# Cutting the last six megabytes of weights into transfers of 120 and of 8 partitions

## The chip, the cores and the metric

The kernel runs on one core of a Trainium2 chip. The metric is the device time of one execution in microseconds (us). A core has five engines that run beside each other: TensorE (PE, matrix products; its weight loads are shown as PEld), VectorE (DVE), ScalarE (ACT), GpSimd (POOL) and SyncE (SP, which here only starts transfers). Transfers between the chip's main memory and the core's own memory of 128 partitions are moved by 16 DMA engines that all transfers share.

## The reference

One inference step of a one-layer backbone over two streams of 128 tokens (T = 256 tokens in all) with model width 1024. The part that matters here is the last one, a mixture of 32 experts, of which every token takes four:

```python
def expert_step(acc, e):
    w_gu_e, b_gu_e, w_down_e, b_down_e, w_tok = e
    g, u = jnp.split(t @ w_gu_e + b_gu_e, 2, axis=-1)
    g = jnp.minimum(g, SWIGLU_LIMIT)
    u = jnp.clip(u, -SWIGLU_LIMIT, SWIGLU_LIMIT)
    act = (u + 1.0) * g * jax.nn.sigmoid(SWIGLU_ALPHA * g)
    out = act @ w_down_e + b_down_e
    return acc + w_tok[:, None].astype(out.dtype) * out, None
```

Each expert has w_gu (1024 by 2048) and w_down (1024 by 1024) in float32, 12 MB together. After the experts come the residual sum and a final norm over the 1024 channels. Before them stands a mixer (a state-space scan and a convolution branch), which the change doesn't touch.

## The kernel before

The mixture of experts takes the last two thirds of the time. The loop `for e in range(NE)` calls `expert(e)` for the 32 experts in order. The order of TensorE's instructions is the order in which the program writes them; the other engines' order is set by a scheduler.

**How an expert's weights come in.** The 12 MB of an expert are six units of 2 MB. Units c = 0 to 3 are 256 rows of w_gu each, units c = 4 and 5 are 512 rows of w_down each. Unit u = 6e + c goes to place u mod 11 of a ring of eleven places (`place`), so the kernel holds nearly two experts at a time. A unit is a tile of 128 partitions by 16 KB: partition p holds k consecutive rows of the matrix (k = 2 for w_gu, 4 for w_down), and `t[:, i]` is the i-th of them. The eleventh place is made of two pieces of 1 MB, whose tiles have names that end in a and b (w_0a, w_0b for unit c = 0); for expert 31 that is unit c = 0.

`load_unit(u, h)` (from line 377) starts the transfers of a unit on SP's queue, line 390. A unit goes as one transfer of 2 MB over all 128 partitions. Only for the last expert (e = 31) a unit of w_down goes as two transfers of 1 MB, each with half of the k rows. `load_pieces` (line 413) calls it for the units that are due: in `expert(e)`, after the second product of expert e - 1 has been written, the units up to number 6e + 10; behind it in the program come a branch (line 1335) to an extra pass for experts with more than 64 tokens of a stream, and the first product of expert e. A transfer can start when the place's last reader is done and when SP has come to it. Each transfer announces its landing on one of eight counters, taken in turn, and SP starts a transfer only when the one that used its counter before has landed.

**What an expert computes.** `expert_up` (line 1224) multiplies the expert's 64 gathered tokens by w_gu: 8 steps k over the 1024 input channels, 8 matmuls in each, so 16 matmuls for a unit, and 4 more for the bias at line 1229. `expert_act` (lines 1237 to 1241, on DVE and ACT) makes the activation, `transposed` (lines 1277 and 1280) turns it, and `down_products` (line 1290) multiplies by w_down: 8 steps of 4 matmuls, step k with row k of the eight that the two w_down units hold on a partition. `keep_y` (line 1298) copies the result out, and products at line 1305 add it to the tokens xT.

For experts 0 to 30 the second product and the adding of a pair are done while the next expert's activation is under way, so TensorE has work in it. After the last expert, `finale` (from line 1456) does what is left: the second product of expert 31, the last adding (lines 1469 and 1168), the squares and their sums, the norm, and five transfers of the output from line 1503.

The lines that the change touches are these of `load_unit`:

```python
        step = k // 2 if e == NE - 1 and c > 3 else k
        for i in range(0, k, step):
            npc_ins[0] = nc.sync.dma_start(t[:, i:i + step], src[:, i:i + step])
        return [t[:, i] for i in range(k)]
```

Of the kernel before, what the change touches and what calls it, by code (L numbers as in the profile page):

```python
# [20 lines left out]
P = 128  # L21
# [4 lines left out]
NE = 32  # L26
# [37 lines left out]
def hybrid_step(ctx, tc, A):  # L64
    nc = tc.nc
# [100 lines left out]
    for i in range(4):  # L166
        r = slice(32 * i, 32 * i + 32)
# [196 lines left out]
    npc_ins, last_early = [None], [None]  # L364
    w_gu, w_dn = A["w_gu"], A["w_down"]

    def place(i, name, h):

        if i < NUNIT - 2:
            return mx[i + 1].tile([P, 4 * D], F32, name=name, tag="w")  # L370
        if i == NUNIT - 2:
            return ypool.tile([P, 4 * D], F32, name=name, tag="y")
        if h:
            return keep.tile([P, 2 * D], F32, name=f"{name}b", tag="xn", bufs=1)
        return mx[0].tile([P, 2 * D], F32, name=f"{name}a", tag="w")

    def load_unit(u, h):

        e, c = divmod(u, 6)
        src, k = (w_gu[0, e, 256 * c:256 * c + 256], 2) if c < 4 else (w_dn[0, e, 512 * (c - 4):512 * (c - 3)], 4)  # L380
        src = src.rearrange("(p k) n -> p k n", k=k)
        t = place(u % NUNIT, f"w{e}_{c}", h)
        if u % NUNIT == NUNIT - 1:
            k //= 2
            src = src[:, h * k:h * k + k]
        t = t.rearrange("p (k n) -> p k n", k=k)

        step = k // 2 if e == NE - 1 and c > 3 else k
        for i in range(0, k, step):
            npc_ins[0] = nc.sync.dma_start(t[:, i:i + step], src[:, i:i + step])  # L390
        return [t[:, i] for i in range(k)]

    def parts(u):
# [6 lines left out]
    def early_pieces(n):  # L400

        with tc.issue_after(last_load[0].ins):
            for _ in range(n):
                u, h = early.pop(0)
                ready[u, h] = load_unit(u, h)
                last_early[0] = npc_ins[0]
# [6 lines left out]
    def load_pieces(n):  # L413

        for u in range(nun[0], min(n, 6 * NE)):
            for h in parts(u):
                pieces.setdefault(u // 6, []).extend(ready.pop((u, h), None) or load_unit(u, h))
        nun[0] = max(nun[0], n)
# [1169 lines left out]
```

## Time and profile before

| | us |
|---|---|
| median of 3 runs | 1441.97 |
| lowest and highest of them | 1440.35 and 1442.50 |
| the profiled execution, its own time | 1441.85 |
| its span, from the first to the last instruction | 1440.0 |

| engine | busy, us | share of the span |
|---|---|---|
| PE | 1341.3 | 93% |
| DVE | 591.6 | 41% |
| ACT | 337.8 | 23% |
| POOL | 110.2 | 8% |

The time of an execution is its span and 1.85 us around it. A busy share is a mean over stages that are limited by different things, so it doesn't tell what a change in one stage is worth: for that, the stretch in which the change lies is looked at, and in it what each wait ends with. Times in the rows below are counted from the start of the span.

### The profile page before, as it was taken

The page shows a single profiled execution, that of the slowest core. Times are in us where ns is not written, and L with a number is a line of the kernel's source. Part 1 is how long each engine was busy: PE and PEld are TensorE (multiplying, and loading weights), DVE is VectorE, ACT ScalarE, POOL GpSimd, SP SyncE. Part 2 cuts the span into 40 slices and gives each one's busy share as a digit, 9 for nine tenths or more (in the row PEclk, how much of TensorE's full clock was granted, in tenths as well). Part 3 has the DMA queues.
Part 4 walks back from the last instruction along what each step waited for, and adds up shares of the span by engine and source line. Part 5 has one row for each costly group of instructions (what it writes and reads, how often), then busy time and mean ns, then how long its engine had stood idle before and what let it go on. Part 6 is the DMA issues. An engine that isn't in the chain of part 4 may idle for free. (4 is left out here: it accounts for less than half of the span.)

```text
span 1440.0 us, 20912 instructions
## 1 busy us (share of the span) xinstructions
PE 1341.3 (93%) x8545; PEld 795.8 (55%) x8545; DVE 591.6 (41%) x1265; ACT 337.8 (23%) x636; POOL 110.2 (8%) x121
## 2 busy tenths in 40 slices
PE   6999999999999899999999899999999999989995
PEld 3888888898999643434434344344333443434432
DVE  4856789898776322123122213213212213123123
ACT  2534565565664100000000001000000010000001
POOL 1112313431002100000000000000000000000001
PEclk9999999999999899999999999999999999999998
DMA  9996666556877799999999999999999999999981
GB/s 367 275 275 175 217 211 236 206 211 205 312 289 264 274 401 425 424 423 426 422 426 425 413 419 425 422 426 425 424 425 424 426 423 427 422 426 424 425 369 37
DMA packets 83711, 506.55 MB, mean 352 GB/s; under 512 B 6866, under 2 KB 34130, under 8 KB 51410
## 3 DMA queue, kind: packets, MB, share of 16 engines
q1 hardware_dynamic: 80658, 497.71, 86.8%
q10 hardware_dynamic: 2880, 6.60, 1.3%
q8 instruction: 100, 1.64, 0.5%
q14 instruction: 73, 0.60, 0.1%
HBM read 498.26 MB, written 5.64 MB: 350 GB/s over the span
## 5 line engine op out<-in xcount | busy, mean ns | idle before, releaser
L291 DVE TENSOR_TENSOR wl<-win,wh 128x1024 fp32r<-128x1024 f32 (+1 forms) x84 | 101.3, 1217 | 36.5 <-ACT wh L290 24.0
L290 ACT CAST wh<-win 128x1024 fp32r<-128x1024 f32 (+1 forms) x84 | 83.9, 1009 | 73.2 <-PE pbc L318 19.2
L1482 POOL TENSOR_TENSOR sql<-sql 128x256 f32<-128x256 f32 x3 | 2.2, 730 | 943.0 <-PE pcl L1469 942.6
L702 POOL TENSOR_TENSOR m<-m_half,adt 128x512 fp32r<-128x512 f32 x32 | 43.2, 1370 | 89.2 <-PE pss L705 89.2
L318 PE MATMUL pxs<-hT,wh 128*128 128x256 f32 x256 | 37.5, 291 | 0.0
L318 PE MATMUL pz<-hT,wh 128*128 128x256 f32 x256 | 37.3, 291 | 0.0
L318 PE MATMUL pgt<-hT,wh 128*128 128x256 f32 x256 | 36.0, 287 | 0.6 <-ACT wh L290 0.6
L318 PE MATMUL pbc<-hT,wh 128*128 128x256 f32 x256 | 35.6, 287 | 0.0
L318 PEld LDWEIGHTS pxs<-hT,wh 128*128 128x128 f32 x256 | 32.5, 190 | 3.6 <-issue 2.8
L318 PE MATMUL pso<-yhl,wh 128*128 128x256 f32 x256 | 34.1, 284 | 0.0
L318 PEld LDWEIGHTS pz<-hT,wh 128*128 128x128 f32 x256 | 33.0, 193 | 1.8 <-issue 1.8
L318 PEld LDWEIGHTS pgt<-hT,wh 128*128 128x128 f32 x256 | 32.4, 191 | 2.6 <-issue 1.9
L318 PEld LDWEIGHTS pbc<-hT,wh 128*128 128x128 f32 x256 | 32.2, 190 | 1.9 <-issue 1.7
L318 PEld LDWEIGHTS pso<-yhl,wh 128*128 128x128 f32 x256 | 32.1, 192 | 0.0
L318 PE MATMUL pglu<-hT,wh 128*128 128x256 f32 x192 | 27.1, 293 | 0.0
L318 PEld LDWEIGHTS pglu<-hT,wh 128*128 128x128 f32 x192 | 25.2, 199 | 0.8 <-issue 0.5
L215 PE MATMUL pm<-ada,sc__170 128*32 128x512 f32 x80 | 15.0, 807 | 9.9 <-DMA ada<-in_w_ada 9.9
L291 DVE TENSOR_TENSOR wl<-wso,wh 128x1024 fp32r<-128x1024 f32 x16 | 19.5, 1221 | 7.5 <-ACT wh L290 7.3
L686 DVE SCALAR_TENSOR_TENSOR gd<-gm,dtT,gd 128x128 f32<-128x128 f32 x64 | 21.3, 381 | 1.7 <-ACT gd L685 1.3
L685 ACT ACTIVATE gd<-gm,dtT 128x128 f32<-128x128 f32 x64 | 20.8, 415 | 4.3 <-DVE gm L676 4.3
L290 ACT CAST wh<-wso 128x1024 fp32r<-128x1024 f32 x16 | 16.7, 1045 | 14.3 <-PE pso L318 10.8
L318 PE MATMUL pwo<-mhl,wh 128*128 128x256 f32 x128 | 18.9, 290 | 0.2 <-DVE mhl L996 0.2
(1094 smaller groups left out, 2640.4 us busy)
## 6 DMA issues: line engine op xcount, KB each, us to landing
w<-in_w_gu SPq DMA_DIRECT2D x116, 2048.0 KB, 30.3
w<-in_w_down SPq DMA_DIRECT2D x57, 2048.0 KB, 26.3
win<-in_w_in_pack SPq DMA_DIRECT2D x38, 1024.0 KB, 5.6
ada<-in_w_ada SPq DMA_DIRECT2D x10, 1024.0 KB, 10.1
wso<-in_w_ssd_out SPq DMA_DIRECT2D x8, 1024.0 KB, 6.8
im<-dru SPq DMA_DIRECT2D x16, 312.0 KB, 9.5
wcf<-in_w_conf_out SPq DMA_DIRECT2D x4, 1024.0 KB, 9.3
wo<-in_w_o SPq DMA_DIRECT2D x4, 1024.0 KB, 9.2
```

Of the source, the lines that this page charges most:

```text
L215: PE.matmul(out[32 * j:32 * j + 32, :], sc_[:, 4 * r + j, 6 - 2 * c:38 - 2 * c], part[:, j, :], start=(start and r == 0), stop=(stop and r ...
L290: S.copy(hi[:, ks, 0:m], w[:, ks])
L291: V.tensor_tensor(lo[:, ks, 0:m], w[:, ks], hi[:, ks, 0:m], ALU.subtract)
L318: last_wo[0] = PE.matmul(out, w[:, k, 0:n], m[:, k, :], start=first and i == 0, stop=last and i == len(order) - 1, skip_group_check=True)
L685: S.activation(gd[s][:, h, :], gm[:, 0, s, :], AF.Copy, scale=dtT[:, 0, s, c0:c0 + 1])
L686: V.scalar_tensor_tensor(gd[s][:, h, :], gm[:, 1, s, :], dtT[:, 0, s, 32 + c0:33 + c0], gd[s][:, h, :], op0=ALU.mult, op1=ALU.add)
L702: G.tensor_tensor(m4[d], m_half[:, d, None, None, :].to_broadcast([P, 2, 4, 64]), ac[d], ALU.mult)
L1482: G.tensor_tensor(sq[:, 0], sq[:, 0], sq[:, k], ALU.add)
```

## The change

For the last three units of expert 31 (c = 3, the last of w_gu, and c = 4 and 5, its w_down: 6 MB) every transfer over 128 partitions is replaced by two: one over partitions 0 to 119, and behind it on the same queue one over partitions 120 to 127. The five transfers of these units become ten. Places, tiles, rows and everything that computes stay as they are.

```diff
         step = k // 2 if e == NE - 1 and c > 3 else k
+
         for i in range(0, k, step):
-            npc_ins[0] = nc.sync.dma_start(t[:, i:i + step], src[:, i:i + step])
+            for r in (slice(0, 120), slice(120, P)) if e == NE - 1 and c > 2 else (slice(0, P),):
+                npc_ins[0] = nc.sync.dma_start(t[r, i:i + step], src[r, i:i + step])
         return [t[:, i] for i in range(k)]
```

## Rows read from the trace of the kernel before

**Rows 1.** Chain that ended last, in order of time: start, us, what.
```profile
1331.39 38.74 DMA w<-in_w_gu
1370.20 35.24 DMA w<-in_w_gu
1405.48 3.65 PE e31pgu L1224 x16
```

**Rows 2.** Timeline of PE, 1360 to 1424: start, us, what, idle before.
```profile
1364.43 14.27 PE L1224 MATMUL e30pgu<-w,xg 128*64 128x512 f32 x64 [0.29 <-PEq L1335]
...
1385.38 7.09 PE L1290 MATMUL e30py<-w,e30aT 128*64 128x512 f32 x32 [0.68 <-ACT e30aT L1280]
...
1394.95 1.91 PE L1224 MATMUL e31pgu<-w_0b,xg 128*64 128x512 f32 x8
1396.66 3.63 PE L1224 MATMUL e31pgu<-w,xg 128*64 128x512 f32 x16
1400.58 3.65 PE L1224 MATMUL e31pgu<-w,xg 128*64 128x512 f32 x16 [0.29 <-DMA w<-in_w_gu]
1405.48 3.65 PE L1224 MATMUL e31pgu<-w,xg 128*64 128x512 f32 x16 [1.25 <-DMA w<-in_w_gu]
...
1412.40 0.72 PE L1277 MATMUL e31pat<-ident,e31gm 128*128 128x128 f32 x4 [2.83 <-DVE e31gm L1241]
1413.80 8.67 PE L1290 MATMUL e31py<-w,e31aT 128*64 128x512 f32 x32 [0.68 <-ACT e31aT L1280]
```

**Rows 3.** Stretches: busy of each engine, PEclk, DMA share, GB/s.
```profile
1223.00:1390.00 167.00, 155.85 (x772) 66.78 (x772) 39.34 (x102) 13.98 (x24) 0.00 (x0) 1.00 1.01 424
...
1394.00:1402.00 8.00, 7.71 (x38) 2.80 (x36) 0.00 (x0) 0.00 (x0) 0.00 (x0) 1.00 0.68 274
1402.00:1404.00 2.00, 2.00 (x12) 0.50 (x8) 0.00 (x0) 0.00 (x0) 0.00 (x0) 1.00 0.20 82
1406.00:1412.00 6.00, 3.57 (x20) 1.06 (x16) 2.41 (x4) 0.63 (x1) 0.00 (x0) 1.00 0.06 26
1414.00:1416.00 2.00, 2.00 (x6) 0.56 (x6) 0.00 (x0) 0.00 (x0) 0.00 (x0) 0.50 0.03 12
```

**Rows 4.** Timeline of SP, 1331 to 1390: the starts of transfers.
```profile
1331.39 2.81 SPq L390 DMA_DIRECT2D w<-in_w_gu  x2
1338.78 6.21 SPq L390 DMA_DIRECT2D w<-in_w_down  x2
1349.56 0.33 SPq L390 DMA_DIRECT2D w_0a<-in_w_gu  x1
1354.47 0.33 SPq L390 DMA_DIRECT2D w_0b<-in_w_gu  x1
1359.37 11.16 SPq L390 DMA_DIRECT2D w<-in_w_gu  x3
1375.06 12.56 SPq L390 DMA_DIRECT2D w<-in_w_down  x4
...
1379.93 0.33 SPq L390 DMA_DIRECT2D w<-in_w_down  x1
1384.99 0.33 SPq L390 DMA_DIRECT2D w<-in_w_down  x1
1387.30 0.33 SPq L390 DMA_DIRECT2D w<-in_w_down  x1
```

**Rows 5.** DMA issues at 1354.47, 1375.06 and 1387.30: KB, us to landing.
```profile
w_0b<-in_w_gu SPq DMA_DIRECT2D x1, 1024.0 KB, 35.3
w<-in_w_down SPq DMA_DIRECT2D x1, 1024.0 KB, 32.9
w<-in_w_down SPq DMA_DIRECT2D x1, 1024.0 KB, 28.1
```

**Rows 6.** DMA issues on an emptier queue: the output's last, and w_in_pack's.
```profile
o_tokens<-xT SPq DMA_DIRECT2D x2, 128.0 KB, 2.0
win<-in_w_in_pack SPq DMA_DIRECT2D x38, 1024.0 KB, 5.6
```

## The prediction

> **What bounds the kernel now.** The chain of waits, read backwards from the end, says that the last thing TensorE (PE) waits for in the expert loop is a transfer: unit c = 3 of expert 31, started at 1370.20 and landed 35.24 us later, at 1405.44, and PE goes on at 1405.48 [rows 1]. From there everything to the end hangs on PE and the short work of the other engines. The timeline of PE shows how little that wait costs: of the four units of w_gu of expert 31, the third makes PE wait 0.29 us (to 1400.58) and the fourth 1.25 us [rows 2]. The second product, e31py, is not waiting for weights at all: it starts at 1413.80 when its input e31aT is ready.
>
> The table of stretches says why that transfer is late [rows 3]. Up to 1390 the 16 DMA engines are full (share 1.01, 424 GB/s, so 26.5 GB/s each). From 1394 to 1402 the share is 0.68, from 1402 to 1404 it is 0.20, and from 1406 to 1412 it is 0.06 at 26 GB/s: one engine out of sixteen, alone. So fifteen engines have carried all their part of the 6 MB by about 1404, and one is more than 11 us behind. A transfer counts as landed when its last engine is done, so the late engine sets every landing. The four transfers of w_down bear this out: the first lands at 1375.06 + 32.9 = 1407.96, the last at 1387.30 + 28.1 = 1415.40 [rows 4, 5]. That is 7.44 us for three more transfers, 2.48 us each; a sixteenth of 1 MB, 65,536 bytes, in 2.48 us is 26.4 GB/s, the speed of one engine. It carries exactly the share of 8 partitions out of 128.
>
> The same rows tell when the fifteen have c = 3. Their slowest ends near 1403.5, and the four transfers of w_down behind c = 3 take 4 x 2.48 = 9.9 us, so c = 3 is done on them by about 1393.6, 11.8 us before it counts as landed.
>
> **The change, part by part.**
>
> *Which engine is relieved.* Eight partitions are one engine's part of 128. If the 120 partitions are carried by fifteen engines, 8 partitions each as now, and the engine left out is the late one, it gets nothing of c = 3, 4 and 5 from those. The other eight partitions of c = 3 are 131,072 bytes. Spread over eight engines that is one partition of 16 KB each, 0.62 us at 26.4 GB/s; carried by one engine it is 4.96 us. The trace of before has no transfer of 8 or of 120 partitions, so I bound both: the landing of c = 3 comes between 1393.6 + 0.6 = 1394.2 (late engine left out, eight rows spread) and 1405.44 + 4.96 = 1410.40 (late engine not left out, and all eight rows on it). I take the lower end: the cut at 120 leaves fifteen whole shares of the kind that the landings show.
>
> [...]
>
> *c = 3 in time.* What PE waits for then is c = 2, a transfer that isn't touched: PE still starts that unit's 16 matmuls at 1400.58. Without a wait a unit takes 16 matmuls at the spacing of the groups before, 1396.66 - 1394.95 = 1.71 us for 8, so 3.42 us [rows 2]. The last unit starts at 1404.00 instead of 1405.48: **-1.48 us**. Landed at 1394.2, it has nearly 10 us to spare.
>
> *The queue of SP.* Transfers take eight counters in turn, and a start waits for the landing of the eighth transfer before it. The chain shows it: the one started at 1331.39 lands at 1370.13, and the next start is 1370.20; from 1331.39 there are 2 + 2 + 1 + 1 + 2 = 8 starts before that [rows 1, 4]. With ten transfers in place of five, the same starts reach less far. 120 of c = 3 starts at 1370.20 as before, its 8 at 1375.06; the first half of c = 4 at 1379.93 and 1384.99, the second at 1387.30 and (landing of w_0b, 1354.47 + 35.3) 1389.8. The first half of c = 5 needs the landings of c = 1 (a 2 MB share, 4.96 us, after w_0b: 1394.8) and of c = 2 (1400.5). Then the last two start behind each other near 1401.2 and 1401.8, since the counters they need, those of c = 3, are free. All of it is late compared with 1375.06 to 1387.30 now. On an emptier queue 1 MB lands in 5.6 us and 128 KB in 2.0 us [rows 6], so the last lands near 1401.2 + 5.6 = 1406.8. The fifteen engines by themselves would need 1403.5 plus an eighth of 14.9 us on those that carry extra rows, 1405.4. So 1407 at the latest.
>
> That is hidden by the first product and the activation: e31py then starts at 1412.3, and its steps 6 and 7, which read the last half, come 6/8 of 7.09 us later, at 1417.6. Ten us of cover. If the cover were gone, each us of delay would be a us of the end. Nobody is queued behind SP's waits but the output's transfers at 1434. Nor does PE wait for SP at the branch of line 1335: PE passed it and began e30pgu at 1364.43, and SP, which has the starts of units 185 to 190 ahead of that branch, did them until 1379.93 [rows 2, 4]. The five added starts cost SP 0.33 us each in time that it spends waiting.
>
> *More waits on PE.* Each of five units has two landings to wait for instead of one; both are long past, and no row shows a price apart from the idle times. Nothing, with 0.1 us each as an upper bound.
>
> *The clock.* [...] So e31py takes 8.67 us where e30py takes 7.09, at full clock: 1.58 us lost [rows 2]. [...] I take the clock to fall as before, because the longest idle is the one that stays; the other end is that the 1.58 us come back as well.
>
> **The sum.** The profiled execution has 1441.85 us, 0.12 below the median of 1441.97. 1441.85 - 1.48 = 1440.37, so **1440.4 us**, 0.1% less. That is within 0.2% (2.9 us), which is about what a measurement of this kernel can tell from no change.
>
> **The rivals.**
>
> *The clock comes back too.* [...] Against it: 2.83 us without a matmul remain. 1440.37 - 1.58 = 1438.8, just past 0.2%.
>
> *Not relieved.* The late engine is one of the fifteen. For it: nothing in the trace names it. Then c = 3 lands at 1405.44 as now and, if the engine also carries one of the eight rows, 0.62 us later, with PE behind it: 1441.9 to 1442.5. The last half would start after that landing and be done near 1417, before 1419.7, when it would be needed. The time doesn't change.
>
> *Slower: fifteen engines that don't reach the pace of sixteen.* Place: the two units of w_down. If a transfer of 120 partitions runs at half speed, then from the slowest engine's start on c = 3 (1393.6 - 4.96 = 1388.6), with 9.9 us for c = 3 and 5.0 for each half, and 0.6 and 0.3 for the small ones, c = 3 is there at 1399.1 (still in time), the halves at 1404.4, 1409.6, 1414.9 and 1420.2. e31py waits for the last and does its last quarter, 1.77 us: 1422.0 against 1413.80 + 8.67 = 1422.47 now. So at half speed the gain is just gone, and slower still costs: at a third of full speed c = 3 comes at 1404.1, the halves every 7.7 us, the last at 1434.9, and the end 14 us later, 1456. Against it: an engine alone moves 26 GB/s, as each does among sixteen, so they don't take from each other now [rows 3]. The same arithmetic gives 1444.6, just past 0.2%, at 0.45 of full speed.
>
> [...]
>
> **Chances.** Forecast 0.64, clock back 0.13, not relieved 0.17, too slow 0.06. Faster by over 0.2% is most of the clock's case and a little of the forecast's, as the three runs lie 2.15 us apart: 0.12. Slower by over 0.2% is the last case: 0.06. Within 0.2% is the rest, 0.82. The range goes from the clock's case to that of no relief with the added row: 1438.6 to 1442.6.
>
> **What would show it.** In the profile after: the idle before the last 16 matmuls of e31pgu gone and that before the group ahead still there, ending near 1400.6; the DMA share falling to 0.06 only before that, and no engine alone after 1407; SP's starts at the times given, the last two past 1400; e31py starting near 1412.3 without a DMA wait. It is wrong if c = 3 still lands after 1404.0 (the wrong engine was relieved), if e31py waits for w_down (too slow), or if PE's clock there is 1.00 (the clock's case).

## The result

The kernel after takes 1464.87 us (median of 4 runs, 1459.46 to 1467.86) against 1441.6 us before (4 runs on the same chip, 1440.35 to 1442.5): ratio 1.0155, 95% interval 1.0132 to 1.0178, so 1.6% **slower**. The forecast was 1440.4 us, in a range of 1438.6 to 1442.6, and no measurable change. The profiled execution of after takes 1465.07 us with a span of 1463.2, 23.2 more than that of before.

The new loop moves the lines behind it by two: L1226, L1292 and L392 of after are L1224, L1290 and L390 of before. The chain that ended last (start, us, what) shows where the time is:

```profile
1357.84 44.47 DMA w_0b<-in_w_gu
...
1402.35 3.34 PE e31pgu L1226 x8
1405.69 7.73 another core or an unknown queue
...
1413.46 5.09 PE e31pgu L1226 x16
1418.55 4.64 another core or an unknown queue
...
1423.23 5.32 PE e31pgu L1226 x16
```

The chain of before has one late transfer at its end, c = 3 [rows 1]. That of after has three, and all three are transfers that the change doesn't touch: w_0b, c = 1 and c = 2. The two stretches of "another core or an unknown queue" are waits for a landing that the chain gives to no instruction; the timeline of PE (start, us, what, and in brackets the idle before it and what ended it) names them:

```profile
1367.18 10.52 PE L1226 MATMUL e30pgu<-w,xg 128*64 128x512 f32 x48 [0.29 <-PEq L1337]
1378.42 3.65 PE L1226 MATMUL e30pgu<-w,xg 128*64 128x512 f32 x16 [0.72 <-DMA w<-in_w_gu]
...
1393.15 3.65 PE L1292 MATMUL e30py<-w,e30aT 128*64 128x512 f32 x16 [0.73 <-DMA w<-in_w_down]
...
1397.54 1.94 PE L1226 MATMUL e31pgu<-w_0a,xg 128*64 128x512 f32 x8
1402.35 3.34 PE L1226 MATMUL e31pgu<-w_0b,xg 128*64 128x512 f32 x8 [2.88 <-DMA w_0b<-in_w_gu]
1413.46 5.09 PE L1226 MATMUL e31pgu<-w,xg 128*64 128x512 f32 x16 [7.78 <-DMA w<-in_w_gu]
1423.23 5.32 PE L1226 MATMUL e31pgu<-w,xg 128*64 128x512 f32 x16 [4.69 <-DMA w<-in_w_gu]
1428.97 3.65 PE L1226 MATMUL e31pgu<-w,xg 128*64 128x512 f32 x16 [0.41 <-DMA w<-in_w_gu]
...
1437.28 8.56 PE L1292 MATMUL e31py<-w,e31aT 128*64 128x512 f32 x32 [0.68 <-ACT e31aT L1282]
```

Read beside [rows 2], the waits before e31pgu are 2.88 + 7.78 + 4.69 + 0.41 = 15.76 us instead of 0.29 + 1.25 = 1.54: +14.22. Behind the three long waits the granted clock is lower as well: the groups of w_0b, c = 1 and c = 2, which took 1.91, 3.63 and 3.65 us at a granted clock of 1.00, take 3.34, 5.09 and 5.32 (clock 0.59 at 1402 to 1406, and 0.50 at 1410 to 1414 and 0.67 at 1424 to 1428 in the table below), together +4.56. With the 0.73 us ahead of the second half of e30py that is 19.51 us.

To keep apart what an execution lost earlier, I take the time from the start of e30pgu to the start of e31py: 1413.80 - 1364.43 = 49.37 us before [rows 2], and 1437.28 - 1367.18 = 70.10 after, +20.73. The other 2.75 us of the profiled execution were lost by 1367.18, ahead of the first changed transfer (SP starts it at 1373.52), so they aren't the change's. Such differences are usual: e30pgu starts between 1360.89 and 1367.18 in the nine traces of this kernel and its variants. Nor is the 0.72 us inside e30pgu the change's: that transfer landed at 1378.38, before the rate of the transfers fell (next table). That leaves 20.0 us, of which 19.51 are named above.

The table of stretches (length, busy of PE, PEld, DVE, ACT, POOL, granted clock, DMA share, GB/s), to be read beside [rows 3]:

```profile
1226.00:1374.00 148.00, 138.90 (x696) 59.37 (x694) 31.61 (x78) 12.77 (x22) 0.00 (x0) 1.00 1.01 425
...
1378.00:1382.00 4.00, 3.58 (x18) 1.27 (x20) 0.00 (x0) 0.00 (x0) 0.00 (x0) 1.00 1.04 440
1382.00:1386.00 4.00, 3.53 (x18) 2.14 (x14) 3.67 (x10) 0.63 (x1) 0.00 (x0) 1.00 1.04 254
1386.00:1390.00 4.00, 2.81 (x14) 1.80 (x16) 4.00 (x15) 0.59 (x1) 0.00 (x0) 1.00 0.90 197
...
1398.00:1402.00 4.00, 1.47 (x8) 0.33 (x4) 0.15 (x1) 0.01 (x1) 0.00 (x0) 1.00 0.94 203
...
1410.00:1414.00 4.00, 0.54 (x2) 0.29 (x4) 0.00 (x0) 0.00 (x0) 0.00 (x0) 0.50 0.64 164
...
1422.00:1424.00 2.00, 0.77 (x2) 0.30 (x4) 0.00 (x0) 0.00 (x0) 0.00 (x0) 0.80 0.07 25
1424.00:1428.00 4.00, 4.00 (x16) 1.12 (x12) 0.00 (x0) 0.00 (x0) 0.00 (x0) 0.67 0.12 39
```

Two columns must be read together here. From 1382 to 1402 the DMA share stays at 0.9 and more, so the engines look about as full as ever, but they move 197 to 254 GB/s instead of the 425 of the first row: the packets take longer. The median packet of 16 KB (one row of a unit) took 0.614 us before, 1.2 us between 1384 and 1423 of after, and 0.617 us from 1424 to 1428 (six packets), when the late engine was nearly alone again (a share of 0.12).

The landings, which the trace keeps one by one (sixteen for a transfer of 128 partitions), say which packets PE waits for (us; "late" is a transfer's last landing, "next" the last but one of its sixteen, or of its fifteen and eight in the last two rows):

```
                        before: next    late   |  after: next     late
w_down, 2nd of e30           1374.01  1384.93  |       1377.60  1393.10
w_0a                         1376.49  1387.28  |       1380.08  1397.08
w_0b                         1378.97  1389.77  |       1382.56  1402.31
c = 1                        1383.88  1394.69  |       1391.83  1413.42
c = 2                        1388.79  1400.54  |       1402.16  1423.19
c = 3 (120 rows in after)    1393.70  1405.44  |       1410.27  1428.22
c = 3, 8 rows                                  |       1409.61  1428.83
```

The late engine stands in every row of after, in the transfer of 120 partitions (15 landings) and in that of 8 (8 landings): their last landings come 5.03 us and 5.64 us behind its c = 2, when the others are done by 1410.27. And its own steps through old, uncut transfers have about doubled: from w_0a to w_0b to c = 1 to c = 2 it takes 5.23, 11.11 and 9.77 us, against 2.49, 4.92 and 5.85. In before the same landings show that the lag has built up slowly: the last engine comes 6.2 us behind the last but one at 1092, 8.9 at 1218, 10.8 at 1395 and 11.8 with c = 2.

The landings also show when this starts and what it isn't. The first five engines have c = 2 at 1382.89 to 1383.61 and come to the cut rows then, just where the GB/s falls; the first four landings of the 120 rows follow at 1392.67 to 1393.04, nearly ten us later, where the same five had taken 4.9 us from c = 1 to c = 2. The late engine hadn't begun on cut rows: its own share of the 120 comes after its c = 2 and takes 5.03 us (1423.19 to 1428.22), the old pace, as the others are nearly done by then. So a share of cut rows isn't slow in itself: packets are slow while many engines carry such shares (1.2 us against 0.617), and those of old transfers are slow with them (11.11 us for c = 1 against 4.92).

### The profile page after: what moved, and what is told of

It reads as the page before. It is cut to its first block, busy times and chain, and to the rows that moved or that the text cites. A ratio compares the mean times of both kernels' runs of the same rounds, so it can differ in the third digit from the quotient of the medians.

```text
span 1463.2 us, 20921 instructions
## 1 busy us (share of the span) xinstructions
PE 1348.1 (92%) x8545; PEld 797.2 (54%) x8545; DVE 589.9 (40%) x1265; ACT 337.7 (23%) x636; POOL 109.8 (8%) x121
## 3 DMA queue, kind: packets, MB, share of 16 engines
HBM read 498.26 MB, written 5.64 MB: 344 GB/s over the span
## 5 line engine op out<-in xcount | busy, mean ns | idle before, releaser
L1226 PE MATMUL e31pgu<-w,xg 128*64 128x512 f32 x48 | 14.1, 738 | 12.9 <-DMA w<-in_w_gu 12.9
L688 DVE SCALAR_TENSOR_TENSOR gd<-gm,dtT,gd 128x128 f32<-128x128 f32 x64 | 21.3, 381 | 1.7 <-ACT gd L687 1.2
L290 ACT CAST wh<-wso 128x1024 fp32r<-128x1024 f32 x16 | 16.7, 1046 | 14.3 <-PE pso L318 10.8
```

The costliest lines, as they stand in the source:

```text
L290: S.copy(hi[:, ks, 0:m], w[:, ks])
L688: V.scalar_tensor_tensor(gd[s][:, h, :], gm[:, 1, s, :], dtT[:, 0, s, 32 + c0:33 + c0], gd[s][:, h, :], op0=ALU.mult, op1=ALU.add)
L1226: PE.matmul(banks[i][m * q:m * q + m, 0:wd], xg[:, k, :], w[k][:, c0:c0 + wd], start=(k == 0), stop=False, skip_group_check=True)
```

## The experiments

Three things changed at once: fifteen and eight engines instead of sixteen (by the landings), ten starts instead of five, and rows cut otherwise. The theory to test is that the cut itself slows the engines, through where the rows go. The rivals are the number of engines, the number of starts and counters, and the addresses that are read.

**bench_rows.** No model at all: thirteen groups of eight loads of 16 KB per partition into one tile, each group after the one before has landed. The outputs are copies of that tile.

```python
buf[:, i] <- src[i][0:128]                  # L82, L85, L118
buf[0:120, i] <- src[i][0:120]              # L88; L91 with 112, L94 with 64
buf[0:120, i] <- far[i][0:120]              # L97; L100 with 128: rows 64 KB apart
buf[0:120, i] <- row[i] to 120 partitions   # L103; L106 with 128: one row, repeated
buf[0:8, i] <- src[i][0:8]                  # L109
buf[0:32:4, i] <- src[i][0:8]               # L112
buf[0:128:16, i] <- src[i][0:8]             # L115
```

> No model at all: thirteen groups of eight loads into one buffer of 128 partitions, each group begun when the one before has landed; 16 KB to a partition in every load; the outputs are copies of the buffer. Groups of 128 rows (2 MB) should take 39.6 us at 26.5 GB/s per engine. [...] Theory B (reading: each engine's source becomes one run of 128 KB in main memory and these collide): 120 contiguous rows about 79 us, but 120 rows from one repeated row about 40 us, and the three groups of eight rows are alike. Theory C (neither; the slow pace is the big kernel's own, from many small starts): 120 rows take 40 us, 112 rows 35 us, 64 rows 20 us.

The timeline of SP gives the start of each group; a group's time is the distance to the next start. Below it, the page's row of GB/s in 40 slices of 15.1 us.

```profile
42.97 4.13 SPq L85 DMA_DIRECT2D buf<-in_w_gu  x8
85.27 3.75 SPq L88 DMA_DIRECT2D buf<-in_w_gu  x8
165.41 3.75 SPq L91 DMA_DIRECT2D buf<-in_w_gu  x8
223.37 5.04 SPq L94 DMA_DIRECT2D buf<-in_w_gu  x8
266.83 3.62 SPq L97 DMA_DIRECT2D buf<-in_w_gu  x8
344.83 3.94 SPq L100 DMA_DIRECT2D buf<-in_w_gu  x8
386.70 3.66 SPq L103 DMA_DIRECT2D buf<-in_w_gu  x8
466.69 4.16 SPq L106 DMA_DIRECT2D buf<-in_w_gu  x8
508.74 2.66 SPq L109 DMA_DIRECT2D buf<-in_w_gu  x8
530.04 5.42 SPq L112 DMA_DIRECT2D buf<-in_w_gu  x8
539.18 4.85 SPq L115 DMA_DIRECT2D buf<-in_w_gu  x8
551.99 4.01 SPq L118 DMA_DIRECT2D buf<-in_w_gu  x8
```

```profile
GB/s 358 429 346 419 431 304 199 207 200 207 165 265 267 265 211 207 206 170 205 207 208 210 168 432 433 301 203 202 205 195 172 412 428 284 49 96 167 432 431 334
```

128 rows take 42.3 us and run at 430 GB/s. 120 rows, less data, take 80.1 us (about 200 GB/s). The source doesn't matter: 120 rows that lie 64 KB apart take 78.0 us, one row sent 120 times 80.0, and the same two with 128 rows 41.9 and 42.05. The number of engines isn't the reason either: 112 rows land with sixteen announcements, as 128 do, and still take 58.0 us (265 GB/s; theory C had 35). 64 rows, half the data, take 43.5 us (206 GB/s). What is left is where the rows go, and which engine carries which. Eight rows from the same source (8 rows posted 8 landings in after) show that the place counts. Into adjacent partitions the eight loads take 21.3 us, into partitions 16 apart 12.8, into partitions 4 apart 9.1. By the landings one load follows another in 2.41 us (131,072 bytes: 54 GB/s) and in 1.29 us (102 GB/s); 4 apart they come as fast as SP starts them, 0.67 us apart.

So the pace depends on which partitions are written: 54 GB/s for eight adjacent ones and 102 for eight that lie 16 apart, from the same rows. And of the four cuts of a unit only that of 128 rows is fast: 430 GB/s, against 200 for 120 rows, 265 for 112 and 206 for 64. Why a place has the pace it has is shown by no run, nor which rows an engine gets of 120 or 112; that such transfers run at 200 and 265 GB/s instead of 430 is measured.

**probe_late.** The kernel before, with eight loads of a few bytes behind the last weights. The 8 rows of after posted 8 landings; if a load of n rows uses n engines, and fewer rows use the first of the same engines, the smallest n with a late landing names the engine. Nothing of the model reads them.

```diff
+        if u == 6 * NE - 1:
+            probe = place((u + 2) % NUNIT, "probe", 0)
+            for j, n in enumerate((7, 4, 2, 6, 1, 3, 5, 8)):
+                nc.sync.dma_start(probe[0:n, 16 * j:16 * j + 16], A["w_dt"][0:n, 0, 0:16])
+                if n > 6:
+                    G.tensor_copy(probe[0:n, 512 + 16 * j:512 + 16 * j + 16], probe[0:n, 16 * j:16 * j + 16])
```

> The kernel before, with eight tiny loads of 7, 4, 2, 6, 1, 3, 5 and 8 rows behind the last weights, into memory that nothing of the model reads, and GpSimd reading the one of 7 and the one of 8 rows. A load of n rows goes over n engines if the changed kernel's landings are read rightly (8 landings for 8 rows). If engines are taken from the lowest number, the late engine is the n-th for the smallest n whose load is late. Theory A (the late engine is the eighth): all loads of 1 to 7 rows land 2 to 3 us after their start, that of 7 near 1392, and only that of 8 comes after the last weights, near 1415. Theory B (one of the first seven): the load of 7 rows is late too, near 1415, and the smaller ones tell which. The time stays within 0.2% of before.

1439.44 us in one execution, with before at 1442.29: the probes cost nothing that shows. The landings of 7, 6, 5 and 4 rows, started at 1387.21, 1402.83, 1410.32 and 1392.06, were complete at 1412.99 to 1413.53, when the late engine had the last weights down (1412.80); those of 3, 2 and 1 rows within 1.4 us of their start. GpSimd's copy behind the 7 rows shows it in its timeline:

```profile
1413.13 0.19 POOL L396 COPY probe<-probe 7x16 f32<-7x16 f32 x1 [931.71 <-DMA probe<-in_w_dt]
```

Four rows are the smallest load that lands late, so, counted that way, the late engine is the fourth, and not the eighth as in theory A. It is among the fifteen and among the eight, as the landings of after show without any counting.

**ten_full.** Ten transfers for c = 3 to 5, like the change, but each over all 128 partitions.

```diff
-        step = k // 2 if e == NE - 1 and c > 3 else k
+        step = 1 if e == NE - 1 and c > 2 else k
```

> Ten transfers for the last three units as in the change, but each of 128 partitions, cut by rows of the matrix (1 MB for c = 3, 0.5 MB for c = 4 and 5). If the price of the change came from ten starts on eight counters: 1455 to 1465. If it came from how 120 and 8 rows lie on engines and partitions: no price, 1440 to 1442, and as c = 3 comes in two halves its wait shrinks, so up to 1.5 us less than before.

Faster by 0.2%: 1438.93 us against 1442.29, ratio 0.9977 [0.9965, 0.9989]; the median is 3.4 us less, more than the 1.5 expected, but the interval reaches down to 1.6. Ten starts and their counters are not the price. In the timeline of PE the wait before c = 3 is gone (32 matmuls in one run), which is the term that the prediction counted on:

```profile
1397.93 7.09 PE L1224 MATMUL e31pgu<-w,xg 128*64 128x512 f32 x32 [0.30 <-DMA w<-in_w_gu]
...
1408.28 1.10 PE L1277 MATMUL e31pat<-ident,e31gm 128*128 128x128 f32 x4 [2.83 <-DVE e31gm L1241]
1410.06 9.16 PE L1290 MATMUL e31py<-w,e31aT 128*64 128x512 f32 x32 [0.68 <-ACT e31aT L1280]
...
1425.68 2.41 PE L196 MATMUL pssl<-one,sql 128*128 128x1 f32 x20 [0.71 <-POOL sql L1482]
```

**c3_halves.** Only c = 3 in two halves over 128 partitions, six starts.

```diff
-        step = k // 2 if e == NE - 1 and c > 3 else k
+        step = k // 2 if e == NE - 1 and c > 2 else k
```

> Before, with unit c = 3 of expert 31 in two transfers of 128 partitions and 1 MB, as its w_down has them already; six starts instead of five. The late engine is left as it is. The first half lands about 2.5 us before the second, the second where c = 3 landed, so TensorE does 8 of the 16 matmuls while it waits: the wait of 1.25 us shrinks to 0.3 us or less. Theory A (the whole gain of the ten transfers is this wait): 1.0 to 1.5 us less than before, ratio 0.9990 to 0.9993, as the ten had within their interval. Rival (w_down in quarters had a share in the gain): no change that shows, ratio 0.9995 to 1.0005.

1440.67 against 1441.61 us, ratio 0.9990 [0.9979, 1.0000]: no difference clear of noise, and the interval holds both what theory A and what its rival expected. The same run of 32 matmuls without a wait stands in its trace, and from e30pgu to e31py it takes 48.37 us, as ten_full takes 48.41: 1.0 less than before.

```profile
1401.19 7.09 PE L1224 MATMUL e31pgu<-w,xg 128*64 128x512 f32 x32 [0.28 <-DMA w<-in_w_gu]
```

**cut_112.** The change with the cut at 112, so that both parts divide by sixteen (112 rows posted sixteen landings in bench_rows).

```diff
-            for r in (slice(0, 120), slice(120, P)) if e == NE - 1 and c > 2 else (slice(0, P),):
+            for r in (slice(0, 112), slice(112, P)) if e == NE - 1 and c > 2 else (slice(0, P),):
```

> The change with the cut at 112 instead of 120: 112 rows are 7 for each of 16 engines, 16 rows are one for each, so no engine is left out and none carries more than its sixteenth. [...] If the price is that fifteen and eight engines are used, unevenly: 1440 to 1443.

1457.25 us in one execution, against 1442.29 of before: not the 1440 to 1443 of a price for using fifteen and eight engines. It is the same picture as the change; first a stretch (1380 to 1384, 209 GB/s), then PE's longest wait, the one before c = 1:

```profile
1380.00:1384.00 4.00, 3.33 (x18) 1.76 (x18) 3.23 (x13) 0.58 (x1) 0.00 (x0) 1.00 1.00 209
```

```profile
1405.85 5.74 PE L1225 MATMUL e31pgu<-w,xg 128*64 128x512 f32 x16 [8.36 <-DMA w<-in_w_gu]
```

**cut_64, c3_only, c5_only.** The same edit with the cut at 64; with the cut at 120 for c = 3 alone (`c == 3`); and for c = 5 alone (`c == 5`), which has no bytes that e31pgu reads.

> The change with the cut at 64: two transfers of 64 partitions each, over 16 engines, four partitions on each. In the load test 64 rows went at 206 GB/s, half of 128 rows. [...]

> The change for unit c = 3 alone; c = 4 and 5 as before. [...] Rival (the price is that of c = 4 and 5 behind it, or of ten starts): 0 to 2 us more. If the late engine had been left out, it would be 1.5 us less.

> The change for unit c = 5 alone, the last 2 MB, for which TensorE doesn't wait in the kernel before. [...] Rival (each transfer of 120 or 8 rows is slow in itself only): c = 5 lands later and nothing waits for it but the last steps of e31py: 0 to 2 us more.

One execution each, beside 1441.61 us of before: 1464.92, 1460.09 and 1451.19, so +23.3, +18.5 and +9.6 us. All three are slower, as they must be if the cut rows slow other transfers, and the 0 to 2 us of the rivals of c3_only and c5_only are out. What sets the three sizes is shown by no run. c5_only is the one that tells most. The stretches show the GB/s fall while c = 1 and c = 2 are on their way, and the timeline of PE shows what it waits before c = 1, c = 2 and c = 3: 7.58 us instead of the 1.54 of [rows 2]. With the 2.92 us that the group of c = 2 takes longer (6.57 instead of 3.65, with the granted clock at 0.50 from 1408 to 1412 and 0.74 from 1412 to 1416) that is the whole difference of 8.9 us in the measure below:

```profile
1384.00:1388.00 4.00, 3.33 (x18) 1.79 (x19) 3.29 (x13) 0.59 (x1) 0.00 (x0) 1.00 1.03 430
1388.00:1392.00 4.00, 4.00 (x20) 1.29 (x18) 0.00 (x0) 0.00 (x0) 0.00 (x0) 1.00 1.04 328
1392.00:1396.00 4.00, 3.85 (x21) 1.50 (x19) 0.69 (x1) 1.16 (x2) 0.00 (x0) 1.00 0.90 205
```

```profile
1399.34 3.65 PE L1225 MATMUL e31pgu<-w,xg 128*64 128x512 f32 x16 [1.87 <-DMA w<-in_w_gu]
1408.14 6.57 PE L1225 MATMUL e31pgu<-w,xg 128*64 128x512 f32 x16 [5.15 <-DMA w<-in_w_gu]
1415.27 3.65 PE L1225 MATMUL e31pgu<-w,xg 128*64 128x512 f32 x16 [0.56 <-DMA w<-in_w_gu]
```

By the landings fifteen engines had c = 1 at 1384.27 and c = 2 at 1389.19, in time; the late one brought them at 1399.29 and 1408.10. That cut rows of c = 5 slow older, uncut rows on another engine is shown by this; where the two meet is not shown. In c3_only the slow time begins earlier and w_0b is hit too:

```profile
1400.23 1.94 PE L1225 MATMUL e31pgu<-w_0b,xg 128*64 128x512 f32 x8 [3.25 <-DMA w_0b<-in_w_gu]
1409.19 8.73 PE L1225 MATMUL e31pgu<-w,xg 128*64 128x512 f32 x32 [7.03 <-DMA w<-in_w_gu]
1421.56 5.35 PE L1225 MATMUL e31pgu<-w,xg 128*64 128x512 f32 x16 [3.65 <-DMA w<-in_w_gu]
```

All in one measure, from the start of e30pgu to that of e31py, worked out from the timelines of PE (us). In brackets stand the waits inside e30pgu, for weights of expert 30 that no edit touches; they differ from trace to trace and are part of the measure:

```
before 49.37 (0)     probe_late 49.85 (0.58)  ten_full 48.41 (0.22)  c3_halves 48.37 (0.20)
after  70.10 (0.72)  cut_112    68.96 (0.18)  cut_64   71.58 (1.26)  c3_only   68.73 (1.62)  c5_only 58.31 (0)
```

Less the brackets, probe_late agrees with before to 0.1 us, and the cuts at 120, 112 and 64 cost 20.0, 19.4 and 21.0: nearly the same, though the times of their single executions lie further apart. c = 3 alone costs 17.7 and c = 5 alone 8.9, so the prices of the units don't add up to that of the change.

## Why the prediction was wrong

*One engine is late and sets each landing.* Right, and the sum used only a part of it: the engine is late in all that is on its queue, not in c = 3 alone (in before 10.8 to 11.8 us in each row of the table of landings).

*Which engine is relieved.* This is the step that failed, twice over. No run shows an engine left out by the cut, on which the -1.48 us rest: the landings of after are fifteen for the 120 rows and eight for the 8, as the step had it, with the late engine among both. It took the late engine for relieved and let c = 3 land at 1394.2, with 1410.40 as the other bound; c = 3 landed at 1428.22 and 1428.83, past both, and past the 1404.0 that it had named as the sign of the wrong engine. First, the cut at 120 leaves the late engine in both parts, as the rival "not relieved" had it. Second, the step took fifteen "whole shares" for fifteen shares at the old pace, and both bounds rest on that pace. But 120 rows run at about half pace even with nothing else under way (200 GB/s against 430 in bench_rows), and in the kernel the median packet took twice as long (1.2 us against 0.614). The late engine pays for this on the bytes that it still has of older transfers: when the GB/s fell, from 1382 on, it had yet to bring the second unit of e30's w_down, w_0a, w_0b, c = 1 and c = 2. The other engines had w_0b at 1382.56, and PE got it at 1402.35. Even with the late engine left out the step wouldn't have held with the traffic as it ran: of the fifteen landings of c = 3's 120 rows the fourteenth came at 1410.27, where 1404.0 was needed (1406.75 on the clock of this execution, which ran 2.75 us later). That last point is argued from the landings; no run left the late engine out.

*The rival on the slower side.* It had the pace, transfers of 120 rows at half speed (200 GB/s against 430), and gave it a chance of 0.06; its place and price were wrong. What spoke against it, that an engine alone moves 26 GB/s as each does among sixteen, was read from transfers over 128 partitions and says nothing of other cuts. It put the loss on w_down and found none at half pace, because it let the late engine be relieved and let c = 1 and c = 2 land as before. In after, e31py waits for no weights at all; the price, 14.22 us of waits and 4.56 of clock, stands in e31pgu.

*c = 3 in time, -1.48 us.* The term holds where c = 3 is in time: in ten_full and c3_halves PE does c = 2 and c = 3 in one run. What it brings up to e31py is less, 1.0 us, or 1.2 without the waits inside e30pgu, mostly for the reason in the next point.

*The clock.* Forecast as falling where it did (0.50 at 1414 to 1416 in before [rows 3]; 0.61 at 1436 to 1440 in after, where e31py takes 8.56 us). In ten_full and c3_halves it is lost one product earlier: e31pat takes 1.10 us instead of 0.72 and e31py 9.16 and 9.18 instead of 8.67. That takes back 0.4 us ahead of e31py and 0.5 in it. So the rival "the clock comes back too" had the sign wrong for these two products: without the idle of 1.25 us before c = 3 the clock fell earlier. That less idle keeps it up is shown by no run, nor why it fell. In the stretch of e31pat it is 0.90 in before (first line) and 0.50 in ten_full (second line):

```profile
1412.00:1414.00 2.00, 0.92 (x6) 0.76 (x8) 0.26 (x1) 0.59 (x1) 0.00 (x0) 0.90 0.06 25
1408.00:1410.00 2.00, 1.10 (x4) 0.73 (x4) 0.14 (x1) 0.58 (x1) 0.00 (x0) 0.50 0.06 25
```

Behind e31py some of it comes back: the sums of squares take 2.41 us in ten_full and 2.86 in before:

```profile
1428.92 2.86 PE L196 MATMUL pssl<-one,sql 128*128 128x1 f32 x20 [0.71 <-POOL sql L1482]
```

In after, the groups behind the waits of 2.88, 7.78 and 4.69 us took 4.56 us more, with the granted clock down to 0.50 (1410 to 1414), which the sum had no term for.

*The queue of SP.* Right in kind: starts of after follow landings (w_0b lands at 1402.31, a start comes at 1402.32), and ten of them cost nothing (ten_full). With landings late they came late as well, the last two at 1428.24 and 1428.85 instead of 1401. The last half of w_down landed at 1442.42; e31py, at 1437.28 + 6/8 of 8.56, needed it at 1443.70. The cover of ten microseconds had shrunk to about 1.3, so that e31py waits for no weights, as forecast, held by little.

*More waits on PE.* Nothing, as taken: ten_full has ten landings to wait for and is faster. The bound of 0.1 us each had no row behind it and is shown by no run; nothing hung on it.

The version that beats both kernels is ten_full, 0.9977 [0.9965, 0.9989]. From the start of e30pgu to the end of the span its trace is 1.3 us shorter than that of before (1.0 less up to e31py, 0.5 more in it, 0.8 less behind it). Where the rest of the 3.4 us between the medians comes from stays open; the interval reaches down to 1.6 us.

## What to carry to other kernels

A transfer's partitions were part of its price here (eight loads of 120 took 80.1 us, of 128 42.3): before cutting one by partitions, measure the cut by itself on an idle core, and cut along the bytes of a partition instead, which cost nothing here with ten starts. When one engine is late, ask first which one it is, with a few tiny loads behind the traffic; and count as exposed everything that still lies on its queue, not only what is being changed. In a table of stretches a full DMA share says only that the engines are occupied, and GB/s beside it whether they get anywhere: in after a share of 0.94 went with 203 GB/s, and one of 1.01 with 425.

## What the runs showed that I had not expected

A load of 1.88 MB took almost twice as long as one of 2 MB: 120 partitions 80.1 us for eight, 128 partitions 42.3. Slow transfers slowed their neighbours: the late engine's share of an uncut unit, 4.92 us for c = 1 before, took 11.11. And the 120/8 cut of one unit out of 192, behind everything that PE was waiting for, cost 9.6 us of 1441.61 in its one execution.
